# Taking every engine's instructions in source order, in a two-layer encoder trunk on one core

## The chip, the cores and the metric

The kernel runs on one core of a Trainium2 chip. The metric is the device time of one execution in microseconds (us): the median of three runs. The profile is of one further execution of the same program. PE is the TensorE matmul engine (PEld its weight loads), DVE VectorE, ACT ScalarE, POOL GpSimd, SP SyncE, which here only issues transfers.

## What is computed

Two layers on 256 tokens of width 2048 in float32. Each layer is a norm, one input projection, eight retention heads and a gated linear recurrence side by side, an output projection, and a SwiGLU feed-forward part of width 5632; a last norm follows.

```python
for l in range(DEPTH):                               # DEPTH = 2
    h = _rmsnorm(x, norm1_g[l])
    p = (h @ w_in[l]).astype(f32)
    q, k, v, g, xb, yb = jnp.split(p, ...)           # 5 x 1024 wide, and yb
    o_ret = _retention(q, k, v, g, ret_gn_g[l])      # 8 heads of 128
    o_lru = _rg_lru_branch(xb, yb, ...)              # conv, gates, scan over time, gelu, norm
    x = x + jnp.concatenate([o_ret, o_lru], -1) @ w_out[l]
    h = _rmsnorm(x, norm2_g[l])
    x = x + (jax.nn.silu(h @ ffn_w_gate[l]) * (h @ ffn_w_up[l])) @ ffn_w_down[l]
return _rmsnorm(x, final_g)
```

## The kernel before

**Split products.** A weight comes from memory as float32 (`raw`, loads of up to 1 MB issued by SP, three buffers). ACT makes of it `whi`, a copy in the engine's reduced format, and DVE makes `wlo = raw - whi` (lines 557 and 558, in `split`). Activations are pairs of the same kind, made by `pair` (lines 126 to 130). A product is then one matmul of 512 columns with `whi` and one of 256 with `wlo` (lines 193 and 195) per piece of 128 of the contraction.

**Units and ticks.** The work is a list of units, one per weight slot, and the loop at the end of `trunk` walks it. In a layer, units 0 to 7 are the v projection, which uses lines 438 to 440. Units 8 to 47 are the other projections, 16 pieces each: for the recurrent channel group n = 0 to 7 its x is unit 8 + 4n and its y unit 9 + 4n, and two units of heads (q, k, g in turn) follow. The heads that are left come after n = 7, so that units 38 to 47 are g4, q5, k5, g5, q6, k6, q7, k7, g6, g7. Units 48 to 63 are the output projection, and the feed-forward part follows in three thirds of gate, up and down units. A unit of four blocks is written like this: at blocks 0, 1 and 2 a third of the split of the unit two further on, then the block's eight matmuls, then a tick; after the last block the unit's `done`. "(25, block 3)" means the tick after block 3 of unit 25.

```python
for b, block in enumerate(u.blocks):
    ...                      # split(n + 2, part) at blocks 0, 1, 2
    block()
    tk.tick()
if u.done:
    u.done()
```

**What follows the stream.** `tk.after(d, fn)` hangs a step of a branch d ticks behind. For a head: `scores` (PE) five ticks after k is done, `decayed` (DVE, writes `sT`) one later, `weighted` (PE) two later, `moments` (DVE, then two operations on POOL) one later, `normed` (DVE, writes `on`) two later, `turned` (PE transposes) two later, `gated` (DVE, ACT, DVE) one later. For a channel group: `x_done` (ACT `low`, DVE `z` and `xb`, ACT `xc`, DVE three times), `gates` (PE) eight ticks later, `decays` (five operations on ACT) one later, `inputs` (DVE) two later; after an odd n `roots` (ACT) for both groups one later and both `scan`s one later, each of DVE operations with a square on ACT between them. `y_done` (DVE, ACT), `cubic` (DVE, ACT) and `gelu` (DVE) hang on the y unit. With the scan of n = 7 come the `sums` of `yr` two ticks later (PE, DVE `rc`, POOL), `rows` four ticks later (DVE `dg`, PE, ACT), and eight `scaled` from six ticks on (each DVE, ACT, DVE). `softplus`, a run of small dependent operations on DVE (lines 567 to 586), is written for tick 29.

**Order.** The framework fixes, when the program is built, in which order each engine takes its instructions. Source order is its priority, but by its own estimate of when operands are there it puts later instructions ahead of those that would wait. Waits between engines are semaphores; on its engine an instruction waits for those before it.

Of the kernel before, what the change touches and what calls it, by code (L numbers as in the profile page):

```python
# [29 lines left out]
GELU = math.sqrt(2.0 / math.pi)  # L30
# [18 lines left out]


class Ticks:
    """Work that follows the stream of large products, some ticks behind."""

    def __init__(self):
        self.now = 0
# [13 lines left out]


class Unit:
    """One slot of a weight: its source, its width, its products, what follows."""

    def __init__(self, src, width, blocks, done=None, begin=None):
        self.src, self.width, self.blocks = src, width, blocks
# [4 lines left out]
@with_exitstack  # L80
def trunk(ctx: ExitStack, tc, a, out):
    nc = tc.nc
    pool = lambda name, bufs, **k: ctx.enter_context(tc.tile_pool(name=name, bufs=bufs, **k))
    const = pool("const", 1)
    raw_p = pool("raw", RAW)
# [12 lines left out]
    def tmp(tag, n=T, dtype=F32):  # L98
        return (two_p if tag in TWO else one_p).tile([P, n], dtype, tag=tag, name=tag)

    def small():
        return sm_ps.tile([P, 512], F32, tag="sm", name="sm_ps")

    # ---- constants and parameters
    par = const.tile([P, NPAR], F32, name="par")
    rot = const.tile([P, 2, T], F32, name="rot")
    ones = const.tile([P, P], F32, name="ones")
# [2 lines left out]
    n4sp = const.tile([P, DEPTH * NL], F32, name="n4sp")  # L110
# [7 lines left out]
    units = []  # L118
    st = {}

    # ---- pieces of the layers
    def pair(x_ap, scale=None):
        """x (times a column or a number) as two float32r parts whose sum is exact."""
        t = op_p.tile([P, 2, T], F32R, tag="op", name="op")
        if scale is None:
            S.activation(out=t[:, 0, :], in_=x_ap, func=AF.Copy)  # L126
            V.tensor_tensor(out=t[:, 1, :], in0=x_ap, in1=t[:, 0, :].bitcast(F32), op=ALU.subtract)  # L127
        else:
            S.activation(out=t[:, 0, :], in_=x_ap, func=AF.Copy, scale=scale)  # L129
            V.scalar_tensor_tensor(  # L130
                out=t[:, 1, :], in0=x_ap, scalar=scale, in1=t[:, 0, :].bitcast(F32),
                op0=ALU.mult, op1=ALU.subtract,
            )
        return t

    def sums(parts, n, key):
        """1 / sqrt(sum over partitions and parts / n + eps), a column for each half of the tokens."""
        ps = small()
        for j in range(2):
            for i, x in enumerate(parts):  # L140
                PE.matmul(ps[:, j : j + 1], lhsT=x[:, j * P : (j + 1) * P], rhs=ones[:, 0:1],
                          start=i == 0, stop=i == len(parts) - 1)
        rc = two_p.tile([P, 2], F32, tag="rc", name="rc")
        V.tensor_scalar(out=rc, in0=ps[:, 0:2], scalar1=1.0 / n, scalar2=EPS, op0=ALU.mult, op1=ALU.add)  # L144
        G.tensor_tensor(out=rc, in0=rc, in1=mhalf, op=ALU.pow)  # L145
        st[key + "c"] = rc

    def spread(key):
        """The same as a row on every partition, in PSUM."""
        dg = one_p.tile([P, 2, P], F32, tag="dg", name="dg")  # L150
        ps = small()
        for j in range(2):
            V.tensor_scalar(out=dg[:, j, :], in0=ident, scalar1=st[key + "c"][:, j : j + 1], scalar2=None, op0=ALU.mult)
        for j in range(2):
            PE.matmul(ps[:, j * P : (j + 1) * P], lhsT=ones, rhs=dg[:, j, :], start=True, stop=True)  # L155
        return ps[:, :T]
# [13 lines left out]
            V.tensor_tensor(out=st[key], in0=st[key], in1=sq, op=ALU.add)  # L170

    def joined_halves(ps):
        """The two halves of a sum of products, added."""
        low, z = tmp("low"), tmp("z")
        S.activation(out=low, in_=ps[:, T : 2 * T], func=AF.Copy)  # L175
        V.tensor_tensor(out=z, in0=ps[:, 0:T], in1=low, op=ALU.add)  # L176
        return z

    def column_unit(src, n_k, operand, done, begin=None, order=None):
        """128 output features, all tokens: n_k pieces of the contraction."""  # L180
        u = Unit(src, n_k * P, [], begin=begin)
        order = order or list(range(n_k))

        def block(i):
            ks = order[i : i + 4]

            def run():
                if i == 0:
                    u.ps = big_ps.tile([P, 512], F32, tag="big", name="acc_ps")
                for k in ks:  # L190
                    w = slice(k * P, (k + 1) * P)
                    x2 = operand(k)
                    PE.matmul(u.ps, lhsT=u.hi[:, w], rhs=x2.rearrange("p a t -> p (a t)"),  # L193
                              start=k == order[0], stop=False)
                    PE.matmul(u.ps[:, T : 2 * T], lhsT=u.lo[:, w], rhs=x2[:, 0, :],  # L195
                              start=False, stop=k == order[-1])
            return run

        u.blocks += [block(i) for i in range(0, n_k, 4)]
        u.done = lambda: done(u.ps)  # L200
        return u

    # ---- retention
    def rotary(ps, name):
        z = joined_halves(ps)
        t, u, o = tmp("rt"), tmp("ru"), tmp(name)
# [7 lines left out]
    def head(l, h):  # L214
        c = {}

        def g_done(ps):
            """2 silu(g) = g (1 + tanh(g / 2))"""
            z = joined_halves(ps)
            V.tensor_tensor(out=z, in0=z, in1=st["rs"], op=ALU.mult)  # L220
            c["g"] = tmp("sg")
            S.activation(out=c["g"], in_=z, func=AF.Tanh, scale=0.5)
            V.scalar_tensor_tensor(out=c["g"], in0=c["g"], scalar=1.0, in1=z, op0=ALU.add, op1=ALU.mult)
            tk.after(1, turned)
# [72 lines left out]

        return q_done, k_done, g_done

    # ---- recurrent branch  # L300
    def lru(l, n):
        c = {}
        i = l * NL + n
# [26 lines left out]
            tk.after(1, decays)  # L330

        def decays():
            """r, i = (1 + tanh(./2)) / 2;  log a = n4sp (1 + tanh);  1 - a^2 = -tanh(log a) (1 + a^2)"""
            r, g, at, tl, w = tmp("lr"), tmp("lg"), tmp("la"), tmp("lt"), tmp("lw")
            n4 = n4sp[:, i : i + 1]
            S.activation(out=r, in_=c["g_ps"][:, 0:T], func=AF.Tanh, scale=0.5, bias=hb[:, 0, i : i + 1])
            S.activation(out=g, in_=c["g_ps"][:, T : 2 * T], func=AF.Tanh, scale=0.5, bias=hb[:, 1, i : i + 1])
            S.activation(out=at, in_=r, func=AF.Exp, scale=n4, bias=n4)
            S.activation(out=tl, in_=r, func=AF.Tanh, scale=n4, bias=n4)
            S.activation(out=w, in_=at, func=AF.Square)  # L340
            c.update(t=tl, g=g, a=at, w=w)
            tk.after(2, inputs)
# [34 lines left out]
            tk.after(1, cubic)  # L377

        def cubic():
            """2 gelu(y) = y (1 + tanh(GELU (y + 0.044715 y^3)))"""  # L380
            y2 = c["y2"]
            V.tensor_scalar(out=y2, in0=y2, scalar1=0.044715, scalar2=1.0, op0=ALU.mult, op1=ALU.add)
            V.tensor_tensor(out=y2, in0=y2, in1=st["y", l, n], op=ALU.mult)
            S.activation(out=y2, in_=y2, func=AF.Tanh, scale=GELU)
            tk.after(1, gelu)

        def gelu():
            y = st["y", l, n]
            V.scalar_tensor_tensor(out=y, in0=c["y2"], scalar=1.0, in1=y, op0=ALU.add, op1=ALU.mult)
# [8 lines left out]

        return x_begin, x_done, y_done

    # ---- norms between the blocks
    def residual(k, ps):
        V.tensor_tensor(out=X[:, k, :], in0=ps[:, T : 2 * T], in1=X[:, k, :], op=ALU.add)  # L403
        V.tensor_tensor(out=X[:, k, :], in0=ps[:, 0:T], in1=X[:, k, :], op=ALU.add)  # L404

    def after_residual(k, nxt, gains):
        """Chunk k of the residual is new: its part of the next norm and operand."""
        accumulate("xa", X[:, k, :], k == 0)
        st[nxt, k] = pair(X[:, k, :], gains(k))
        if k == KD - 1:  # L410
            tk.after(2, lambda: sums([st["xa"]], D, "rs"))
            tk.after(4, lambda: rows("rs"))
# [5 lines left out]
        st["rot"] = r  # L418

    def v_units(l):  # L420
        """All tokens of half of v, 4 pieces of the contraction to a slot."""
        res = []
        for g in range(2):
            hold = {}
# [35 lines left out]
    def layer_units(l):  # L460
# [12 lines left out]
            for _ in range(REC_AFTER[n] if n < NL - 1 else len(heads)):  # L473
                res.append(heads.pop(0))

        # output projection; the last head is the last to be ready
        order = [0, 1, 2, 3, 4, 5, 6] + list(range(8, 16)) + [7]
        for n in range(KD):
            def done(ps, n=n):
# [11 lines left out]
                u.split_at = (4, 4, 4)  # L491
            res.append(u)

        # feed-forward
        for t, (f0, nf) in enumerate(THIRDS):
            for f in range(f0, f0 + nf):
                c = {}
# [32 lines left out]
    for l in range(DEPTH):  # L530
        units += layer_units(l)
# [31 lines left out]
    sp = [const.tile([P, nl], F32, name=f"sp{j}") for j in range(4)]  # L563

    def softplus():
        """-4 softplus(-lam), with log1p(e) = 2 artanh(e / (2 + e))"""
        lam = par[:, i0 : i0 + nl]
        V.tensor_scalar(out=sp[0], in0=lam, scalar1=-1.0, scalar2=None, op0=ALU.mult)
        V.tensor_tensor(out=sp[1], in0=sp[0], in1=lam, op=ALU.max)
# [14 lines left out]
            b0 = PARAMS[name][0]  # L584
            V.tensor_scalar(out=hb[:, j, :], in0=par[:, b0 : b0 + nl], scalar1=0.5, scalar2=None, op0=ALU.mult)

    # the first operands come with the first weights, a quarter at a time
    V.memset(ones, 1.0)
    V.memset(mhalf, -0.5)
    warm = small()  # L590
# [68 lines left out]


def _columns(w, k0=0, nk=None):
    """[L, K, N] -> [L, N / 128, 128 (k in its piece), pieces * 128]"""
    L, K, N = w.shape
    w = w.reshape(L, K // P, P, N // P, P)[:, k0 : (k0 + nk if nk else None)]
    w = w.transpose(0, 3, 2, 1, 4)
    return np.ascontiguousarray(w).reshape(L, N // P, P, -1)
# [48 lines left out]
```

## Time and profile before

| | us |
|---|---|
| median of three runs | 2266.14 (2265.61 to 2266.22) |
| profiled execution, its span | 2262.9 |
| PE busy in the span | 2239.7 (99%) |
| DVE busy | 1530.3 (68%) |
| ACT busy | 1160.7 (51%) |
| POOL busy | 85.3 (4%) |
| memory traffic | 186 GB/s over the span |

The profiled execution's own time is its span and what lies around it. The span is 3.2 us under the median of the runs. Busy times come from one execution; idle times carry the engine or transfer that ended them. The ends of matmuls are modelled by the profiler, so that starts are the safer numbers on PE.

### The profile page before, as it was taken

How to read it: one execution, taken by the hardware profiler on the slowest of the kernel's cores; microseconds unless marked ns; L12 is line 12 of the kernel's file. 1: busy time of each engine (PE TensorE's matmuls, PEld its weight loads, DVE VectorE, ACT ScalarE, POOL GpSimd, SP SyncE). 2: the span in 40 equal slices, each digit the busy share in tenths (PEclk: the TensorE clock that was granted, in tenths of full speed). 3: DMA queues.
4: the chain of work that ended last, by engine and by line, in shares of the span. 5: the costliest groups of instructions: out<-in, count | busy, mean ns of one | idle time of the engine just before them, and what ended most of it. 6: DMA issues, size and time to landing. Idle time of an engine off the chain costs nothing.

```text
span 2262.9 us, 32580 instructions
## 1 busy us (share of the span) xinstructions
PE 2239.7 (99%) x12748; PEld 1949.9 (86%) x12748; DVE 1530.3 (68%) x2818; ACT 1160.7 (51%) x2040; POOL 85.3 (4%) x128
## 2 busy tenths in 40 slices
PE   8999999999999999999999999999999999999997
PEld 6888888888888888888888888888888888888886
DVE  8788877666566666666758889776665666566665
ACT  5666644555344543445546765455543455444553
POOL 4001110000000000000000101000000000000000
PEclk9999999999999999999999999999999999999999
DMA  7455455555555555555555554555555555555553
GB/s 254 176 177 197 179 177 186 187 192 192 188 189 189 192 185 198 186 189 184 191 200 179 180 192 168 180 186 188 195 184 194 187 190 192 185 196 186 189 182 114
DMA packets 63721, 422.96 MB, mean 187 GB/s; under 512 B 7376, under 2 KB 8016, under 8 KB 25168
## 3 DMA queue, kind: packets, MB, share of 16 engines
q1 hardware_dynamic: 61200, 414.60, 51.7%
q0 software_dynamic: 1792, 5.24, 0.8%
q8 instruction: 99, 1.62, 0.3%
q10 hardware_dynamic: 576, 1.05, 0.1%
q14 instruction: 54, 0.44, 0.1%
HBM read 418.77 MB, written 2.10 MB: 186 GB/s over the span
## 4 chain that ended last, share of the span: by engine, by line
PE 97%; DVE 1%; DMA 1%; issue 0%; POOL 0%; ACT 0%; SPq 0%; DVEq 0%; POOLq 0%
PE acc_ps L193 61%; PE acc_ps L195 31%; PE v_ps L439 1%; PE v_ps L438 1%; PE v_ps L440 1%; PE sm_ps L328 1%; DVE wlo L558 1%; DMA x<-in_x_dram 0%; PE sm_ps L237 0%; DVE op L130 0%; DMA raw<-in_w_v_dram 0%; PE sm_ps L155 0%; PE sm_ps L286 0%; DVE x L642 0%; PE sm_ps L238 0%
## 5 line engine op out<-in xcount | busy, mean ns | idle before, releaser
L193 PE MATMUL acc_ps<-op,whi 128*128 128x512 f32 x6016 | 2105.6, 396 | 0.0
L195 PE MATMUL acc_ps<-op,wlo 128*128 128x256 f32 x6016 | 1672.9, 278 | 0.0
L193 PEld LDWEIGHTS acc_ps<-op,whi 128*128 128x128 f32 x6016 | 1128.8, 188 | 263.3
L558 DVE TENSOR_TENSOR wlo<-raw,whi 128x683 fp32r<-128x683 f32 (+5 forms) x1204 | 1007.5, 851 | 458.4 <-ACT whi L557 457.4
L557 ACT ACTIVATE whi<-raw 128x683 fp32r<-128x683 f32 (+5 forms) x1204 | 860.8, 754 | 853.3 <-PE acc_ps L193 765.7
L195 PEld LDWEIGHTS acc_ps<-op,wlo 128*128 128x128 f32 x6016 | 1131.5, 188 | 0.7
L403 DVE TENSOR_TENSOR x<-acc_ps,x 128x256 f32<-128x256 f32 x128 | 54.3, 424 | 219.1 <-PE acc_ps L195 219.1
L176 DVE TENSOR_TENSOR z<-acc_ps,low 128x256 f32<-128x256 f32 x256 | 107.1, 419 | 2.2 <-ACT low L175 2.2
L175 ACT ACTIVATE low<-acc_ps 128x256 f32<-128x256 f32 x256 | 93.9, 367 | 9.2 <-PE acc_ps L195 9.2
L126 ACT ACTIVATE op<-mix 128x256 fp32r<-128x256 f32 x104 | 43.4, 417 | 71.9 <-DVE mix L507 68.9
L502 ACT ACTIVATE sg<-z 128x256 f32<-128x256 f32 x88 | 36.8, 418 | 67.5 <-DVE z L501 67.5
L145 POOL TENSOR_TENSOR rc<-rc,mhalf 128x2 f32<-128x2 f32 x7 | 7.7, 1096 | 1684.8 <-DVE rc L144 1684.8
L439 PE MATMUL v_ps<-wlo,op 128*128 128x512 f32 x128 | 52.3, 409 | 7.5 <-DVE wlo L558 7.5
L404 DVE TENSOR_TENSOR x<-acc_ps,x 128x256 f32<-128x256 f32 x128 | 54.3, 424 | 4.3
L438 PE MATMUL v_ps<-whi,op 128*128 128x512 f32 x128 | 51.6, 407 | 1.2 <-ACT op L129 1.2
L440 PE MATMUL v_ps<-whi,op 128*128 128x512 f32 x128 | 51.7, 404 | 0.1
L127 DVE TENSOR_TENSOR op<-mix,op 128x256 fp32r<-128x256 f32 x104 | 43.5, 419 | 0.2
L439 PEld LDWEIGHTS v_ps<-wlo,op 128*128 128x128 f32 x128 | 25.3, 197 | 15.0 <-DVE wlo L558 10.1
L506 DVE TENSOR_TENSOR sg<-sg,rs 128x256 f32<-128x256 f32 x88 | 36.9, 420 | 0.8 <-ACT sg L502 0.8
L507 DVE TENSOR_TENSOR mix<-z,sg 128x256 f32<-128x256 f32 x88 | 36.9, 419 | 0.0
L501 DVE TENSOR_TENSOR z<-z,rs 128x256 f32<-128x256 f32 x88 | 36.9, 419 | 0.0
L130 DVE SCALAR_TENSOR_TENSOR op<-x,par,op 128x256 fp32r<-128x256 f32 x64 | 34.3, 539 | 0.2 <-ACT op L129 0.2
(114 smaller groups left out, 729.5 us busy)
## 6 DMA issues: line engine op xcount, KB each, us to landing
raw<-in_w_gate_dram SPq DMA_DIRECT2D x88, 1024.0 KB, 4.8
raw<-in_w_up_dram SPq DMA_DIRECT2D x88, 1024.0 KB, 4.8
raw<-in_w_in_dram SPq DMA_DIRECT2D x80, 1024.0 KB, 4.8
raw<-in_w_down_dram SPq DMA_DIRECT2D x64, 960.0 KB, 4.7
raw<-in_w_out_dram SPq DMA_DIRECT2D x32, 1024.0 KB, 4.8
raw<-in_w_down_dram SPq DMA_DIRECT2D x32, 896.0 KB, 4.5
raw<-in_w_v_dram SPq DMA_DIRECT2D x12, 1024.0 KB, 4.7
raw<-in_w_v_dram SPq DMA_DIRECT2D x16, 256.0 KB, 6.5
```

What stands on the lines that cost most here:

```text
L127: V.tensor_tensor(out=t[:, 1, :], in0=x_ap, in1=t[:, 0, :].bitcast(F32), op=ALU.subtract)
L175: S.activation(out=low, in_=ps[:, T : 2 * T], func=AF.Copy)
L176: V.tensor_tensor(out=z, in0=ps[:, 0:T], in1=low, op=ALU.add)
L193: PE.matmul(u.ps, lhsT=u.hi[:, w], rhs=x2.rearrange("p a t -> p (a t)"), start=k == order[0], stop=False)
L195: PE.matmul(u.ps[:, T : 2 * T], lhsT=u.lo[:, w], rhs=x2[:, 0, :], start=False, stop=k == order[-1])
L403: V.tensor_tensor(out=X[:, k, :], in0=ps[:, T : 2 * T], in1=X[:, k, :], op=ALU.add)
L404: V.tensor_tensor(out=X[:, k, :], in0=ps[:, 0:T], in1=X[:, k, :], op=ALU.add)
L438: PE.matmul(ps, lhsT=x2[:, 0, t], rhs=u.hi[:, w], start=k == 0, stop=False)
L439: PE.matmul(ps, lhsT=x2[:, 0, t], rhs=u.lo[:, w], start=False, stop=False)
L440: PE.matmul(ps, lhsT=x2[:, 1, t], rhs=u.hi[:, w], start=False, stop=k == KD - 1)
L557: S.activation(out=u.hi[:, w], in_=u.raw[:, w], func=AF.Copy)
L558: V.tensor_tensor(out=u.lo[:, w], in0=u.raw[:, w], in1=u.hi[:, w].bitcast(F32), op=ALU.subtract)
```

## The change

One line enters a mode of the framework in which no engine's instructions are reordered: each engine gets them in the order in which the source emits them. Semaphores, buffers, operations and their operands stay. The rest of the diff takes out comments and docstrings.

```diff
 def trunk(ctx: ExitStack, tc, a, out):
     nc = tc.nc
+    ctx.enter_context(tc.manual_schedule())
     pool = lambda name, bufs, **k: ctx.enter_context(tc.tile_pool(name=name, bufs=bufs, **k))
     const = pool("const", 1)
     raw_p = pool("raw", RAW)
```

## Rows read from the trace of the kernel before

**Rows 1.** The page, busy time of each engine (share of the span, instructions).
```profile
PE 2239.7 (99%) x12748; PEld 1949.9 (86%) x12748; DVE 1530.3 (68%) x2818; ACT 1160.7 (51%) x2040; POOL 85.3 (4%) x128
```

**Rows 2.** PE's waits: line, releaser, us in total, times, longest.
```profile
PE v_ps L439 <- DVE wlo L558: 7.5, 6, 3.8
```

**Rows 3.** Four stretches: length, busy us of each engine, clock, DMA.
```profile
16.35:36.70 20.35, 14.09 (x48) 10.18 (x48) 20.21 (x33) 9.83 (x19) 16.44 (x19) 0.83 0.56 197
...
64.80:310.70 245.90, 245.18 (x1414) 214.01 (x1413) 207.14 (x431) 157.78 (x281) 24.19 (x39) 1.00 0.52 182
310.70:2236.00 1925.30, 1924.58 (x11034) 1679.67 (x11034) 1263.40 (x2274) 966.85 (x1696) 29.53 (x43) 1.00 0.53 187
...
143.30:287.80 144.50, 143.78 (x830) 125.25 (x828) 126.16 (x272) 96.28 (x174) 15.91 (x25) 1.00 0.50 178
```

**Rows 4.** PE in order of time: start, us, line, tiles [idle before].
```profile
70.41 0.40 PE L193 MATMUL acc_ps<-op,whi 128*128 128x512 f32 x1
...
143.25 0.48 PE L193 MATMUL acc_ps<-op,whi 128*128 128x512 f32 x1
...
265.19 0.61 PE L141 MATMUL sm_ps<-ones,acc 128*128 128x1 f32 x4
...
287.27 0.30 PE L286 MATMUL sm_ps<-ident,on 128*128 128x128 f32 x1 [0.72 <-DVE on L272]
...
322.37 0.40 PE L193 MATMUL acc_ps<-op,whi 128*128 128x512 f32 x1
...
328.02 0.40 PE L193 MATMUL acc_ps<-op,whi 128*128 128x512 f32 x1
```

**Rows 5.** DVE in order of time, 149 to 173 us.
```profile
149.92 0.87 DVE L558 TENSOR_TENSOR wlo<-raw,whi 128x682 fp32r<-128x682 f32 x1 [0.22 <-ACT whi L557]
150.71 0.42 DVE L176 TENSOR_TENSOR z<-acc_ps,low 128x256 f32<-128x256 f32 x1
...
154.77 0.43 DVE L389 SCALAR_TENSOR_TENSOR y<-y,y 128x256 f32<-128x256 f32 x1 [0.48 <-ACT y L384]
...
157.68 0.42 DVE L208 TENSOR_TENSOR rt<-z,rotl 128x256 f32<-128x256 f32 x1
...
159.00 0.43 DVE L346 SCALAR_TENSOR_TENSOR lg<-lg,xc 128x256 f32<-128x256 f32 x1
...
161.85 0.42 DVE L358 TENSOR_TENSOR lg<-lg,lw 128x256 f32<-128x256 f32 x1
162.31 0.69 DVE L360 TENSOR_TENSOR_SCAN lr<-la,lg 128x256 f32<-128x256 f32 x1
...
171.70 1.53 DVE L319 SCALAR_TENSOR_TENSOR xc<-xb,par,xc 128x256 f32<-128x256 f32 x3
```

**Rows 6.** ACT in order of time, 154 to 159 us.
```profile
154.32 0.42 ACT L384 ACTIVATE y<-y 128x256 f32<-128x256 f32 x1 [1.23 <-DVE y L383]
...
156.58 0.47 ACT L336 ACTIVATE lr<-sm_ps,hb 128x256 f32<-128x256 f32 x1
...
158.59 0.77 ACT L557 ACTIVATE whi<-raw 128x683 fp32r<-128x683 f32 x1
```

**Rows 7.** POOL in order of time, the two operations between `moments` and `normed`.
```profile
284.70 1.13 POOL L264 TENSOR_SCALAR ve<-mv 128x2 f32<-128x2 f32 x1 [7.15 <-DVE mv L262]
285.92 0.76 POOL L265 TENSOR_TENSOR ve<-ve,mhalf 128x2 f32<-128x2 f32 x1
```

**Rows 8.** PE in order of time around its longest idle time.
```profile
19.48 0.80 PE L439 MATMUL v_ps<-wlo,op 128*128 128x512 f32 x1 [3.83 <-DVE wlo L558]
...
20.92 0.63 PE L440 MATMUL v_ps<-whi,op 128*128 128x512 f32 x1
...
25.02 0.39 PE L439 MATMUL v_ps<-wlo,op 128*128 128x512 f32 x1
```

**Rows 9.** ACT and DVE in order of time near the start.
```profile
12.52 0.63 ACT L557 ACTIVATE whi<-raw 128x512 fp32r<-128x512 f32 x1 [0.77 <-DMA raw<-in_w_v_dram]
...
24.15 0.71 DVE L578 TENSOR_SCALAR sp<-sp 128x16 f32<-128x16 f32 x1
```

## The prediction, made before the change was run

> **What bounds the kernel now.** I read the page's busy line first, then PE's waits, then the table of two long stretches, then the engines' instructions in order of time. PE is busy 2239.7 of 2262.9 us, DVE 68%, ACT 51% [rows 1]. PE's own waits add up to little: 7.5 us for `wlo`, all of it at the start [rows 2], 0.72 us a layer for one transpose [rows 4], and some in the tail. So time can only come out of the start; anywhere else the change can at best cost nothing. The reader should see how unlike the two main stretches are [rows 3]. While the projections with their branches run (64.8 to 310.7, and its twin in layer 2), DVE is busy 207.1 of 245.9 us (84%) and ACT 157.8. From there to 2236 DVE has 66%, and in that share lies the whole feed-forward part. An order that makes DVE and ACT wait for each other has room in the second and almost none in the first.
>
> **What the change moves.** No operation is added. On PE nearly nothing moves: the small products already stand at the block ends where the source has them, in both layers, but for three places in each: the sums of `yr` one product into unit 41 (the source: after block 2 of unit 40, nine products earlier), their spread in two pieces in unit 41, and the transposes of head 5 three and five products late, after a wait of 0.72 us [rows 4]. SP issues only weights, in source order already. What moves is DVE and ACT. Today a third of a split slips in between any two dependent steps of a branch. In the source the order in a unit is fixed: third 0, the ticks' work of block 0, third 1, ticks, third 2, ticks, ticks, the unit's `done`. Where a step goes DVE, ACT, DVE, the next `whi` is queued on ACT behind the step that waits for DVE, and DVE's next `wlo` behind that.
>
> **The prices** (DVE's time to get past each piece, start to start, its waiting included). DVE: a third of `wlo` 0.78; a 256-column operation 0.34 where the next is independent, 0.46 where it needs the result; the three of a rotary 1.32, with `z` in front (0.46) and the last (0.34) 2.12; the convolution's three 1.53; a scan 0.72 with its dependent successor; a hop between engines 0.03 [rows 5]. ACT: a `whi` 0.77, a 256-column operation 0.42 of which 0.31 pass before the next may start (my reading of neighbouring starts), the five of `decays` 2.01 [rows 6]. So DVE result, ACT operation, `whi`, `wlo` costs DVE 0.03+0.31+0.77+0.03 = 1.14 of waiting. From these:
> L (third of a split) 0.78; Q (`done` of q or k) 2.12; X (`done` of x: 0.46+0.45+0.63 for ACT's `xc`+1.53) 3.1; Y (`done` of y, wait for `whi` included) 2.02; C (`cubic`: 0.3+0.45+1.14) 1.88; e (`gelu`) 0.34; G (`done` of g) 2.02; P (`gated`: 0.48+1.14) 1.62; M (`moments`) 0.75; N (`normed`) 0.65, 0.5 more where it waits for POOL's two operations of 1.13 and 0.76 [rows 7]; D (`whi` behind `decays` after G) 1.9; I (`inputs`) 0.68; W (`decayed`) 0.47; S (both scans with their squares on ACT, 2×2.41, and 0.36 for `whi`) 5.2; R (`z` behind `roots` on ACT) 0.65; K (one `scaled`: 0.45+0.45+0.34) 1.24.
>
> **The sum for a layer.** Unit by unit in source order, in us:
> 21 X+M+N+3L+0.5: 7.3; 22 Y+C+P+3L: 7.9; 23 Q+I+3L: 5.1; 24 R+Q+S+3L: 10.3; 25 X+W+3L: 5.9; 26 Y+C+e+M+N+3L: 8.0; 27 G+D+P+I+3L: 8.6; 28 Q+3L: 4.5; 29 X+3L: 5.4; 30 Y+C+e+3L: 6.6; 31 as 23: 5.1; 32 R+G+S+W+3L: 10.7; 33 to 35 as 21 to 23: 20.3; 36 as 28: 4.5; 37 as 25: 5.9; 38 as 26: 8.0; 39 as 27: 8.6; 40 as 24 with 0.1 for `rc`: 10.4; 41 Q+3L, `dg` 0.5, 1.7 behind `rs`, 2K: 9.1; 42 G+W+3L+4K: 9.8; 43 Q+M+N+3L+2K: 8.3.
> Together 170.3, and 0.4 for the first `low`: 170.7 us from the start of unit 21 to head 5 being ready for the transposes in unit 44. PE starts unit 21 at 143.25 and has passed these transposes at 288.0, its wait of 0.72 included [rows 4]; at the place where the source has them it is some 142.7 us after 143.25. DVE and ACT are therefore late by 28.0 us. Units 9 to 20 by the same pieces come to 76.4 us; PE takes 143.25-70.41 = 72.8 [rows 4]: 3.6 us more. A lead of two units (5.65 us each [rows 4]) hides lateness of the splits, but not of results that a small product needs two blocks later, so PE stops there. At `weighted` of head 2, the end of unit 25: `decayed` is done after 0.4+7.3+7.9+5.1+10.3 and X+2L+W = 5.1, so at 36.1; PE is there after five units, some 1.9 of small products and 0.7 of waiting for the transposes in unit 22, so at 30.8; it waits 5.3. The same count run on gives 5.6 at `weighted` of head 3 (end of 32), 8.1 at the sums of `yr` (unit 40), 2.3 at their spread, 5.0 at the transposes in unit 44, and some tenths at those of other heads. After that the chain is back within PE's time. 32 us a layer, 64 in all.
> The check on it: DVE is busy 126.2 of 144.5 us there today [rows 3]. The pieces hold that work and some 45 us of waits, where 18 are free.
>
> **The clock.** After PE's longest idle time, 3.83 us, the records of the products last 0.63 us instead of 0.39 until about 23.9 [rows 8], and the granted clock of that stretch is 0.83 on the mean [rows 3]: 4.4 us at the lower of its two levels (1.2 of 2.4 GHz), so 2.2 us lost. Four of the waits are longer. After three of them DVE and ACT are the bound and take the loss in; after the last it counts: 2 us a layer.
>
> **The start.** `softplus` is written for tick 29 but fills DVE from 5.4 us on. From 16.35 to 36.7, where PE last waits, DVE is busy 20.2 of 20.35 us [rows 3], and eleven of those small operations take 4.6 us of it, start to start (one stands in the rows) [rows 9]. Until 16.35 they also kept DVE from unit 1, whose first `whi` was done at 13.15 [rows 9]: 3.1 us more. Against that, PE must still take its products for each of the last pieces, and POOL's sums slow DVE there as before. I take 5 us; between 2 (only the stalls after 16.35 shrink, and the low clock stays) and 7.7. In its own place, unit 7, `softplus` costs some 29 times 0.23 us on a DVE that needs 2.4 of each 5.5 us there: hidden by the lead, which would have to be under 10 us to show it.
>
> **What stays.** In the feed-forward units the same counting gives 4.8 us for a gate and 5.1 for an up, against 5.65 of PE; for the last third's down products 4.9 against 4.94: no loss. The three spreads of `rs` may each make PE wait some 0.3 us: 1 us. The tail, from 2249, is already in source order.
>
> **Rivals.** (1) *The waits mostly overlap*: ACT runs ahead further than I let it, and DVE stops only where even a punctual DVE is late. At the sums: R+Q+L+4.82 = 8.4 us after the start of unit 40, when PE gets there after 4.24: 4.1; the spread 2.3; the transposes 8.34-7.06 (a unit and a block of PE) = 1.3. That is 7.7 a layer: 2266.1+15.4-5+1 = 2277. For it: DVE's plain work fits. (2) *Faster*: the lead covers everything, only the start changes: 2266.1-5 = 2261; it decides if DVE is never more than two blocks (2.8 us) late. Against it: unit 40 alone breaks that. The Trainium skill (Perfetto Trace Analysis, "Identifying the Most-Contended Engine") has one look for the engine with the highest occupancy and work on that first; by that rule PE, whose work stays as it is, would hold the time at this rival's. The rows bear it out for today's order only: DVE's 84% [rows 3] leaves 39 us a layer, and the waits of source order ask for more. (3) *Nothing much moves*, because source order and today's differ too little, or gain and loss cancel: 2266. Against it: DVE's rows show thirds between nearly all dependent steps. (4) *Worse*: the low clock after each wait also falls on PE-bound stretches (four times 2.2 a layer) and the down units with 0.04 us to spare fall behind: 2330+14+16 = 2360.
>
> **How the numbers follow.** The profiled execution's span is 2262.9 us, 3.2 under the median of 2266.14, so the sum is put on the median: 2266.1 + 2×(32+2) - 5 + 1 = 2330. The pieces are good to some 5%, 12 us a layer, since small errors of a sum close to PE's time come out whole. Chances: forecast (2300 to 2350) 0.66; rival (1) 0.15; (2) 0.06; (3) 0.03; (4) 0.10. The range from 2277 to 2360 leaves out (2), (3), and the ends of (1) and (4). A difference of 0.2%, about 4.5 us, is what a measurement of this kernel can tell from none. Slower by more 0.90, within 0.04, faster 0.06.
>
> **What would show it.** In the changed profile: PE waiting for `sT`, `acc`, `dg` and `on` at the places named, in both layers; a granted clock under full in those slices; DVE idle before `wlo` with ACT's `whi` as releaser inside 64 to 350; ACT idle before `sq`, the tanh and `op`, released by DVE; no change in feed-forward; the `softplus` lines after 50 us and `wlo` no longer holding PE at 28 and 36 us. The forecast is wrong if PE shows no wait at the sums of `yr`, or if feed-forward units are longer than 5.65.

## The result, and the profile after

The changed kernel takes 2359.62 us (median of four runs, 2358.17 to 2360.14) against 2265.9 for the kernel before: a ratio of 1.0412, with a 95% interval from 1.0397 to 1.0427. The profiled execution's span is 2357.8 us, 94.9 more than before. Slower, as forecast, but by 94 us and not by 64. Line numbers are one higher than in the kernel before.

The busy line of the page answers [rows 1]. PE has the same 12748 instructions and is busy 37.7 us longer: its records are longer, not more. DVE's 69 us more are not more work. Its 2818 records add up to 1701 us before and 1705 now (`wlo` lasts 851 ns on the mean before and 855 now). Busy time counts records that overlap once, and they overlap less when DVE stands still between two of them. ACT even has 16 instructions fewer: 20 loads of function tables (ACT_TABLE_LOAD, 1.28 us each, which no line of the source names) in place of 36. Eight of the 16 that are gone stood before the square roots of `roots`, which now come in pairs. So the loss is not in the amount of work of any engine.

```profile
PE 2277.4 (97%) x12748; PEld 1968.1 (83%) x12748; DVE 1599.5 (68%) x2818; ACT 1142.0 (48%) x2024; POOL 81.5 (3%) x128
```

PE's waits (line, releaser, us in total, times, longest) answer [rows 2]. The wait for `wlo` at the start has gone; DVE's results of the branches have come in its place.

```profile
PE sm_ps L252 <- DVE sT L245: 27.7, 8, 5.9
PE sm_ps L142 <- DVE acc L171: 17.3, 2, 8.7
PE sm_ps L287 <- DVE on L273: 7.9, 2, 4.0
PE sm_ps L238 <- DVE kT L212: 5.9, 2, 3.0
PE sm_ps L156 <- DVE dg L154: 4.9, 4, 1.8
```

PE in order of time, layer 1 (start, us, line, tiles, idle before). Eight waits stand where [rows 4] has a single one, of 0.72. Layer 2 has them again, each within 0.7 us of layer 1 but for the second, which is 1.98 there (the last row).

```profile
136.64 0.76 PE L238 MATMUL sm_ps<-qT,kT 128*128 128x256 f32 x2 [2.87 <-DVE kT L212]
...
143.71 0.38 PE L252 MATMUL sm_ps<-v,sT 128*128 128x128 f32 x1 [0.37 <-DVE sT L245]
...
180.82 0.80 PE L252 MATMUL sm_ps<-v,sT 128*128 128x128 f32 x2 [5.92 <-DVE sT L245]
...
182.91 0.63 PE L194 MATMUL acc_ps<-op,whi 128*128 128x512 f32 x1
...
185.23 0.39 PE L194 MATMUL acc_ps<-op,whi 128*128 128x512 f32 x1
...
230.22 0.58 PE L252 MATMUL sm_ps<-v,sT 128*128 128x128 f32 x1 [4.91 <-DVE sT L245]
...
289.49 0.56 PE L142 MATMUL sm_ps<-ones,acc 128*128 128x1 f32 x2 [8.67 <-DVE acc L171]
...
296.94 0.38 PE L156 MATMUL sm_ps<-dg,ones 128*128 128x128 f32 x1 [1.82 <-DVE dg L154]
...
311.36 0.49 PE L252 MATMUL sm_ps<-v,sT 128*128 128x128 f32 x2 [1.72 <-DVE sT L245]
...
323.26 0.79 PE L287 MATMUL sm_ps<-ident,on 128*128 128x128 f32 x2 [4.04 <-DVE on L273]
...
1316.26 0.38 PE L252 MATMUL sm_ps<-v,sT 128*128 128x128 f32 x1 [1.98 <-DVE sT L245]
```

The eight of layer 1 sum to 30.3 us. Behind a wait of 5.92 the products of 512 columns last 0.63 us, and 0.39 again from 185.2 on, as in [rows 8].

Four stretches answer [rows 3] (length; busy us and instructions of PE, PEld, DVE, ACT and POOL; granted clock of PE; DMA share and GB/s): the start, units 8 to 47 of layer 1, and the feed-forward products of layer 1 and of layer 2.

```profile
16.00:36.70 20.70, 18.28 (x66) 11.64 (x67) 20.70 (x23) 11.78 (x22) 18.02 (x21) 1.00 0.60 222
...
65.91:356.72 290.81, 260.49 (x1424) 225.03 (x1423) 220.06 (x441) 146.98 (x272) 21.74 (x38) 0.94 0.45 156
...
447.00:1187.80 740.80, 740.80 (x4196) 642.40 (x4195) 477.36 (x792) 350.09 (x613) 0.00 (x0) 1.00 0.54 186
...
1617.47:2344.30 726.83, 726.83 (x4197) 635.38 (x4195) 465.47 (x771) 347.75 (x607) 0.00 (x0) 1.00 0.53 184
```

The two feed-forward stretches hold the same products, at full clock and without idle time of PE, and yet differ by 13.9 us. Before, both took 726.9. In layer 1 the pairs of a 512- and a 256-column product now follow each other at 353.3 ns, in layer 2 at 346.7 as before; 2096 pairs make 13.9 us of it.

Start by start of the units against the trace before: the start gives back 4.5 us; units 8 to 47 take 43.4 more in layer 1 and 41.7 in layer 2; the feed-forward part of layer 1 with its spread 14.4; the feed-forward part of layer 2 nothing. That sums to 95.0 of 94.9.

How a wait arises is seen in unit 22, DVE and then ACT in order of time. DVE's `y` is done, ACT squares it and only then makes the next `whi`, and DVE stands for 1.15 us before `wlo`. Two steps later the same happens with ACT's tanh. The prediction had 1.14 for such a step.

```profile
152.34 0.43 DVE L375 TENSOR_TENSOR y<-z,rs 128x256 f32<-128x256 f32 x1
153.91 0.87 DVE L559 TENSOR_TENSOR wlo<-raw,whi 128x682 fp32r<-128x682 f32 x1 [1.15 <-ACT whi L558]
...
155.02 0.42 DVE L384 TENSOR_TENSOR y<-y,y 128x256 f32<-128x256 f32 x1
156.60 0.87 DVE L559 TENSOR_TENSOR wlo<-raw,whi 128x683 fp32r<-128x683 f32 x1 [1.15 <-ACT whi L558]
```

```profile
152.80 0.42 ACT L377 ACTIVATE y<-y 128x256 f32<-128x256 f32 x1 [2.02 <-DVE y L375]
153.12 0.76 ACT L558 ACTIVATE whi<-raw 128x682 fp32r<-128x682 f32 x1
155.48 0.42 ACT L385 ACTIVATE y<-y 128x256 f32<-128x256 f32 x1 [1.60 <-DVE y L384]
155.80 0.76 ACT L558 ACTIVATE whi<-raw 128x683 fp32r<-128x683 f32 x1
```

### The profile page after: what moved, and what is told of

The parts are those of the page before. It is cut to its first block, busy times and chain, and to the rows that moved or that the text cites. A ratio compares the mean times of both kernels' runs of the same rounds, so it can differ in the third digit from the quotient of the medians.

```text
span 2357.8 us, 32550 instructions
## 1 busy us (share of the span) xinstructions
PE 2277.4 (97%) x12748; PEld 1968.1 (83%) x12748; DVE 1599.5 (68%) x2818; ACT 1142.0 (48%) x2024; POOL 81.5 (3%) x128
## 4 chain that ended last, share of the span: by engine, by line
PE 83%; DVE 10%; ACT 5%; issue 1%; DMA 0%; POOL 0%; SPq 0%; DVEq 0%; ACTq 0%
PE acc_ps L194 53%; PE acc_ps L196 26%; DVE wlo L559 4%; ACT whi L558 2%; PE v_ps L441 1%; PE v_ps L440 1%; PE v_ps L439 1%; DVE z L177 1%; DVE lr L361 0%; DVE op L131 0%; DVE xc L320 0%; ACT L354 0%; DVE y L363 0%; DMA raw<-in_w_v_dram 0%; DVE ru L211 0%
## 5 line engine op out<-in xcount | busy, mean ns | idle before, releaser
L194 PE MATMUL acc_ps<-op,whi 128*128 128x512 f32 x6016 | 2134.1, 400 | 0.0
L559 DVE TENSOR_TENSOR wlo<-raw,whi 128x683 fp32r<-128x683 f32 (+5 forms) x1204 | 970.0, 855 | 235.2 <-ACT whi L558 233.8
L558 ACT ACTIVATE whi<-raw 128x683 fp32r<-128x683 f32 (+5 forms) x1204 | 830.1, 748 | 239.5 <-PE acc_ps L194 185.6
L170 ACT ACTIVATE sq<-x 128x256 f32<-128x256 f32 x59 | 24.7, 418 | 143.2 <-DVE x L405 143.2
L171 DVE TENSOR_TENSOR acc<-acc,sq 128x256 f32<-128x256 f32 x73 | 31.1, 426 | 38.8 <-ACT sq L170 38.8
```

The costliest lines, as they stand in the source:

```text
L558: S.activation(out=u.hi[:, w], in_=u.raw[:, w], func=AF.Copy)
L559: V.tensor_tensor(out=u.lo[:, w], in0=u.raw[:, w], in1=u.hi[:, w].bitcast(F32), op=ALU.subtract)
```

## The experiments

The long spacing comes and goes between runs of one and the same program in six of the kernels below: their times stand in steps of about 14 us. Each layer with the long spacing adds 13.9, so times are compared at the short spacing in both layers; which spacing a run had is shown for the profiled one and inferred from its step for the others. The changed kernel itself is 2359.6 - 13.9 = 2345.7 by that measure, 80 over the kernel before.

### Which engine's order costs the time

```diff
-    ctx.enter_context(tc.manual_schedule())
+    ctx.enter_context(tc.manual_schedule(engines={mybir.EngineType.PE}))
```

> Only PE takes its instructions in source order; DVE, ACT, POOL and SP are ordered as before. Theory (the time goes where DVE and ACT wait for each other): PE's order differs from that of before in three places a layer, and only the sums of yr come early for their operand: in the kernel before DVE finished acc at 265.1 us, and nine products earlier is about 263.7, so 1.4 us a layer, about 1 more for the spread and the transposes: 2266 + 2x2.4 = 2271 (2266 to 2276). Rival (it is PE's own order that costs: a small product at the head of PE's queue holds the large ones behind it): most of the 94 us, so 2330 to 2360.

Measured 2272.02, ratio 1.0027 (1.0016 to 1.0037): 6 us. PE waits 3.2 us for `acc` and 3.0 for `on`. The rival falls.

The same line with `DVE`, with `Activation`, and with both. The engines that are not named, POOL among them, are ordered by the framework.

> Only DVE takes its instructions in source order; ACT, PE and POOL are ordered by the framework. Theory (both engines in source order wait for each other): ACT can put whi ahead of steps that wait for DVE, as in the run with all whi at block 0, so 2305 to 2330 at the short spacing of the feed-forward products, up to 28 more at the long one. Rival (DVE's order alone is the whole cause): 2345 at the short spacing. Rival (ACT's order is the whole cause): 2262 to 2275.

Runs of 2283.01, 2296.30, 2309.53 and 2310.60, ratio of the median 1.015 (1.0091 to 1.021); the profiled run (2310.60) has the long spacing in both layers. At the short one: 2283, 17 us over the kernel before. That lies between the expectations, under the theory's 2305 and over the 2275 of the rival that lays everything on ACT.

> Only ACT takes its instructions in source order; DVE, PE and POOL are ordered by the framework. At the short spacing of the feed-forward products both engines in source order cost some 58 us (2324, PE ordered by the framework) and DVE alone 17 (2283). Theory (each engine's order is cheap while the other can step around it, and the cost comes from the two together): 2264 to 2290, and 13.9 more for each layer at the long spacing. Rival (the costs add up, and most is ACT's): 17 + x = 58, so 2266 + 41 = 2307, 2300 to 2315.

Eight runs from 2269.17 (profiled, short in both layers) to 2300.57, in three steps; ratio 1.0098 (1.0062 to 1.0134). At the short spacing 3 to 7 us. The theory holds: no engine's order alone costs most of the 80.

> DVE and ACT take their instructions in source order, PE and POOL are ordered by the framework. Theory: the waits stay, because what PE waits for is late, and PE can only put a few large products ahead of a late small one: 2340 to 2360, with the waits for sT, acc, dg and on at the same places. Rival (PE's own order costs): 2262 to 2280.

One run of 2323.98 (profiled, short in both layers) and four of 2351.85 to 2352.80; ratio 1.0382 (1.0365 to 1.0399). At the short spacing 58 us, against 17 and about 5 for the two alone. The places were expected wrongly: with PE ordered by the framework the waits are no longer at the small products. PE's waits of that run:

```profile
PE acc_ps L196 <- DVE wlo L559: 16.9, 22, 1.9
PE acc_ps L194 <- ACT whi L558: 14.7, 10, 3.1
PE sm_ps L142 <- DVE acc L171: 5.8, 2, 3.1
```

PE puts large products ahead of a late small one, until the next split is late as well. The last step, to PE (and POOL) in source order as well, is worth 22 of the 80 us. DVE and ACT alone come to 20 to 24; together they cost 58, so 34 to 38 us exist only when both stand in line for each other. PE's order costs 6 alone and 22 on top of both; PE with only one of the two was not run.

### Is it `whi` behind a step that waits for DVE?

```diff
-        S.activation(out=u.hi[:, w], in_=u.raw[:, w], func=AF.Copy)
+        for p in range(parts) if parts == 3 and part == 0 else [part] if parts != 3 else []:
+            h = slice(p * u.width // parts, (p + 1) * u.width // parts)
+            S.activation(out=u.hi[:, h], in_=u.raw[:, h], func=AF.Copy)
```

> Source order on all engines, but the three whi thirds of a split are written at block 0, one after the other, and only the wlo thirds stay at blocks 0, 1 and 2. Theory (DVE is late because its wlo waits for a whi that is queued on ACT behind a step that waits for DVE): at C, P, D and similar steps some 1.1 us of DVE waiting goes, about 15 to 20 times between unit 21 and unit 44, so 17 to 22 of the 28 us of lateness; the waits in the layers fall from 31 us to under 12 each, and the clock loss with them: 2290 (2275 to 2310). Rival (DVE is late by its own dependent steps and by its plain load, ACT is no part of it): 2355 to 2365, the waits as they are.

Runs of 2324.58, 2337.73, 2351.07 and 2353.92 (profiled, long in both layers); ratio 1.0335 (1.028 to 1.0389). At the short spacing some 2325, about 20 less than the changed kernel's 2345.7. Both expectations miss: the effect is there, at about a third of its size. The groups of DVE's instructions between 143.7 and 310 us (busy, mean ns, idle before and its releaser), of the changed kernel, of this one, and, up to 290 us, of the one with DVE alone in source order, tell why:

```profile
L559 DVE TENSOR_TENSOR wlo<-raw,whi 128x683 fp32r<-128x683 f32 (+1 forms) x66 | 55.5, 865 | 19.2 <-ACT whi L558 19.2
L177 DVE TENSOR_TENSOR z<-acc_ps,low 128x256 f32<-128x256 f32 x22 | 9.2, 419 | 7.1 <-ACT low L176 6.8
```

```profile
L561 DVE TENSOR_TENSOR wlo<-raw,whi 128x683 fp32r<-128x683 f32 (+1 forms) x67 | 56.1, 863 | 6.7 <-ACT whi L560 6.7
L177 DVE TENSOR_TENSOR z<-acc_ps,low 128x256 f32<-128x256 f32 x22 | 9.3, 421 | 12.4 <-ACT low L176 12.1
```

```profile
L559 DVE TENSOR_TENSOR wlo<-raw,whi 128x683 fp32r<-128x683 f32 (+1 forms) x65 | 54.3, 862 | 0.0
L177 DVE TENSOR_TENSOR z<-acc_ps,low 128x256 f32<-128x256 f32 x21 | 8.7, 416 | 3.0 <-ACT low L176 3.0
```

With the three `whi` in a row DVE waits 12.5 us less for `whi` but 5.3 more for `low`, which now stands behind them on ACT. With DVE and ACT in source order and PE free, the two waits add up to 23.4 us over the same work (21.6 and 1.8), much as in the changed kernel; with ACT free too they are 3.0. So it is an ACT that may choose which nearly empties both.

### One lateness or several waits?

```diff
-            tk.after(2, weighted)
+            tk.after(5 if h in (2, 3) else 2, weighted)
```

> Source order on all engines; weighted of heads 2 and 3, and what hangs on it, three ticks (4.2 us) later. Theory (one lateness of DVE and ACT that PE pays in instalments wherever it has to wait): the waits for sT of 5.9 and 4.9 us a layer fall under 2 each, and the wait at the sums of yr grows from 8.7 to 16 to 20; time 2350 to 2361. Rival (each wait is a cost of its own, from a step written too close behind its operand): 10.8 us a layer and the slow clock behind them go, nothing grows: 2330 (2325 to 2338).

2360.37 (three runs of 2359.5 to 2360.4, one of 2373.35), ratio 1.0431 (1.04 to 1.0461): the same as the changed kernel, and the rival falls. PE's waits:

```profile
PE sm_ps L287 <- DVE on L273: 26.1, 6, 5.1
PE sm_ps L142 <- DVE acc L171: 17.3, 2, 8.7
PE sm_ps L252 <- DVE sT L245: 9.4, 6, 2.3
```

Of the 27.7 us for `sT` 18.3 are gone, and `on` has grown by 18.2. The theory holds for the sum, not for the place: the next step of the same heads took the waits over, long before the sums of `yr`, which stay at 8.7.

### What does the clock cost?

```diff
+    def filler(ps, n):
+        for _ in range(n):
+            PE.matmul(ps[:, 0:P], lhsT=ones, rhs=ones, start=True, stop=True)
...
+            filler(ps, {2: 26, 3: 21}.get(h, 0))
```

The last line stands in `weighted`; `sums` of `yr` has 38 of them and `turned` of head 5 has 16.

> Source order on all engines, and PE's four long waits of each layer are filled with products of ones by ones that wait for nothing (26 ahead of weighted of head 2, 21 of head 3, 38 of the sums of yr, 16 of the transposes of head 5; 0.21 us each in the first row of such products, so 5.5, 4.5, 8.1 and 3.4 us), written into the bank that the small products behind them write over. Theory A (the clock that falls after each wait costs PE's time): the granted clock stays at full level in these stretches and about 10 us a layer come back: 2340 (2333 to 2345). Theory B (DVE and ACT set the time up to the transposes in unit 44, and PE's slow products lie inside what it would wait anyway): the clock stays up as well, but PE waits longer behind the filler at the next place, and the time stays at 2355 to 2363.

Runs of 2335.52, 2349.45, 2349.72 and 2363.57 (profiled, long in both layers); ratio 1.0349 (1.0312 to 1.0386). At the short spacing 2335.5: 10 us better than the changed kernel, between A and B. Two stretches of this kernel (columns as above), from unit 21 to the transposes of head 5 and around `weighted` of head 2, and the same two of the changed kernel:

```profile
144.96:319.00 174.04, 167.26 (x1026) 147.00 (x1024) 132.72 (x271) 90.52 (x169) 13.69 (x24) 1.00 0.42 148
180.00:190.00 10.00, 9.91 (x63) 8.71 (x62) 7.56 (x18) 4.38 (x7) 2.26 (x5) 1.00 0.40 137
```

```profile
144.40:323.30 178.90, 151.82 (x824) 131.09 (x822) 132.98 (x272) 91.00 (x169) 13.70 (x24) 0.92 0.42 144
181.00:191.00 10.00, 10.00 (x49) 8.88 (x50) 7.01 (x17) 4.85 (x9) 2.24 (x5) 0.80 0.48 145
```

The granted clock is full in both, and from unit 21 to the transposes PE needs 174.0 us and not 178.9. Three small products of this kernel in order of time say where the gain arises:

```profile
230.64 0.49 PE L258 MATMUL sm_ps<-v,sT 128*128 128x128 f32 x2 [1.45 <-DVE sT L250]
...
287.80 0.38 PE L147 MATMUL sm_ps<-ones,acc 128*128 128x1 f32 x2
...
318.97 0.65 PE L294 MATMUL sm_ps<-ident,on 128*128 128x128 f32 x2 [0.45 <-DVE on L279]
```

Behind `weighted` of head 3 comes DVE's `z` of unit 33, in the changed kernel and in this one:

```profile
239.90 0.42 DVE L177 TENSOR_TENSOR z<-acc_ps,low 128x256 f32<-128x256 f32 x1 [1.41 <-ACT low L176]
```

```profile
238.84 0.41 DVE L182 TENSOR_TENSOR z<-acc_ps,low 128x256 f32<-128x256 f32 x1
```

At `weighted` of head 3 nothing is gained (230.64 against 230.22): what the full clock gave in unit 26 is waited for there, as theory B has it. From there on PE's slow products count, as A has it. To the sums it is 57.2 us instead of 59.3: in the changed kernel DVE stands 1.41 us at 239.90 for a unit that PE ran slowly, and here it does not. From the sums to the transposes it is 31.2 us instead of 33.8; in that part DVE itself needs the spread, the scores and `weighted` from PE. Up to the output projection the two layers gain 6.4 and 4.4 us.

### What sets the spacing of the feed-forward products?

```diff
+        for _ in range(fill):
+            PE.matmul(ps[:, 0:P], lhsT=ones, rhs=ones, start=True, stop=True)
         for j in range(2):
             PE.matmul(ps[:, j * P : (j + 1) * P], lhsT=ones, rhs=dg[:, j, :], start=True, stop=True)
```

`fill` is 8 in the spreads of `rs` and 0 in that of `yr`.

> Source order on all engines; eight products of ones by ones stand ahead of the spread of rs, so that PE has no wait between the large products before it and the spread's four products. Theory (the spacing of the 2096 pairs of feed-forward products is set by the instant at which PE restarts after its wait at that spread; without a wait it is always the short one): 346.7 ns in both layers, the feed-forward stretch of layer 1 726.9 us instead of 740.8: 2346 (2343 to 2348) in every run. Rival (the spacing does not hang on that wait): 353.3 ns in layer 1 as before, or runs that differ by steps of 14.

2351.88, all four runs within 2350.91 to 2352.73; ratio 1.038 (1.0362 to 1.0399). The two feed-forward stretches of this kernel:

```profile
448.60:1175.50 726.90, 726.90 (x4196) 635.71 (x4195) 477.10 (x792) 349.99 (x613) 0.00 (x0) 1.00 0.54 189
1608.71:2335.60 726.89, 726.89 (x4197) 635.73 (x4195) 465.35 (x771) 347.54 (x607) 0.00 (x0) 1.00 0.52 183
```

The theory holds for the spacing: 13.9 us are back, and the steps between runs have gone. The time misses its range of 2343 to 2348. Most of that is the fillers' own cost, 1.5 to 1.6 us at each of the three spreads of `rs` from 400 us on, which nothing hides. The spread of `rs` ahead of the feed-forward part, in the kernel before (layer 1), in the changed one (both layers), and in this one:

```profile
407.57 0.61 PE L155 MATMUL sm_ps<-dg,ones 128*128 128x128 f32 x4
```

```profile
446.53 0.71 PE L156 MATMUL sm_ps<-dg,ones 128*128 128x128 f32 x4
...
1617.00 0.71 PE L156 MATMUL sm_ps<-dg,ones 128*128 128x128 f32 x4
```

```profile
448.24 0.61 PE L158 MATMUL sm_ps<-dg,ones 128*128 128x128 f32 x4
```

Where the four products last 0.61 us, nothing held the first one, and the spacing was short, at all 14 such spreads of the seven profiles that have them. Where they last 0.71, PE seems to have been held at the first of them, too shortly to be listed as a wait (DVE worked on `dg` up to 446.67 in layer 1, past the start of the four); both spacings followed, as here in the two layers, the long one at 8 of 14 such spreads. What decides between them was not found.

Two further runs put products of ones by ones behind the last head's transposes, in the kernel with only its start in source order (below).

```diff
             for j in range(2):
                 PE.transpose(ps[:, j * P : (j + 1) * P], c["on"][:, j, :], ident)
+            for _ in range(2 if h == NH - 1 else 0):
+                PE.matmul(ps[:, 256:384], lhsT=ones, rhs=ones, start=True, stop=True)
```

> The kernel with only units 0 to 7 in source order, and two products of ones by ones of 128 columns behind the last head's transposes, ahead of the first 244 pairs of the output projection. Theory (what stands ahead of the first pair sets the spacing of all pairs up to the next small product): the pairs may go from 353.3 to 346.7 ns, so 244 x 6.6 ns = 1.6 us less a layer against 0.2 for the products: 2258.4 (2257.5 to 2259.5); if the two leave the instant at the same point of the pattern, 353.3 ns stays and it is 2261.7. Rival (the spacing belongs to the output projection's operands): 353.3 ns with any number of products.

> As with two extra products, but four, so that the last four small products are as many and as wide as those of the spread behind which the pairs go at 346.7 ns. Theory: 346.7 ns in the first 244 pairs of the output projection of both layers, 2261.3 - 2x(1.6 - 0.45) = 2259.0 (2258 to 2260). Rival (the spacing belongs to the output projection's operands): 353.3 ns, 2262.2.

2262.0 and 2263.13 (ratios 0.9983, 0.9974 to 0.9993, and 0.9988, 0.9978 to 0.9998). The 244 pairs behind them stay at 353.3 ns, 86.5 us in either, and the products cost 0.7 and 1.9 us. So products put there do not change it. The rival falls too: in the run with ACT alone in source order the same pairs of layer 2 went at 346.7.

### The start, and the feed-forward part alone

```diff
+    order = ExitStack()
+    order.enter_context(tc.manual_schedule())
...
     for n, u in enumerate(units):
+        if n == 8:
+            order.close()
```

> Source order on all engines up to the end of unit 7, then the framework's order as before. Theory: the start gains 4.5 us as in the changed kernel and the rest is as before: 2261.5 (2259 to 2264), PE without the waits for wlo at 28 and 36 us. Rival (the gain of the start is given back later, since PE is then ahead of DVE): 2265 to 2267. If the feed-forward pairs of products lock to the longer spacing in a layer, that layer adds 14.

2261.26, ten runs from 2259.97 to 2262.45, ratio 0.9979 (0.997 to 0.9989). The start's gain stays, and this kernel beats both.

```diff
+        if n in (8, 208):
+            order.close()
+        if n in (66, 266):
+            order.enter_context(tc.manual_schedule())
```

Units are counted through both layers here; the mode is closed again ahead of the tail.

> Source order on all engines everywhere but in units 8 to 65 of each layer (the projections with their branches, the output projection and the first gate and up unit, with the spread of rs), where the framework orders as before; it also orders the tail. Theory (all of the loss arises in units 8 to 47, and the feed-forward part loses only by the spacing that PE takes up at that spread): feed-forward units as before, 346.7 ns in both layers, and the start's 4.5 us gained: 2261.5 (2259 to 2264) in every run. Rival (source order makes DVE or ACT late in feed-forward units too): PE waits for wlo there, 2265 to 2290.

2261.31, ratio 0.998 (0.997 to 0.9989), ten runs within 2 us, both feed-forward parts at 346.7 ns, and no wait of PE for `wlo`. In the feed-forward units source order costs nothing.

## Why the prediction was right and wrong

Of the 31 us by which the span grew more than forecast, 13 are the spacing in the feed-forward part, 10 the pieces and 7 the clock (each beyond what the forecast had for it). That 2359.62 lies inside the outer range, which ends at 2360, is luck: the long spacing came in one layer, and no sum of the prediction had it. Without it the time is 2345.7, inside the forecast's 2300 to 2350.

**Right: the kind and the places of the waits.** `weighted` of head 2: 5.3 forecast, 5.92 measured; of head 3: 5.6 and 4.91; sums of `yr`: 8.1 and 8.67; their spread: 2.3 and 1.82; transposes in unit 44: 5.0 and 4.04; units 9 to 20: 3.6 and 3.24, before `scores` and `weighted` of head 1. Only the 1.72 before `weighted` of head 5 was put among the tenths. Together 30.3 against 32 a layer. The start: 5 forecast, 4.5 measured, with the clock full from 16 to 36.7 us, where [rows 3] has 0.83, and `softplus` from 56.6 us on. The rivals "waits mostly overlap", "faster" and "nothing" fall: PE waits at every place named.

**Mis-sized: the clock, 2 us a layer.** Filling the four long waits gave 6.4 us back in layer 1 and 4.4 in layer 2. The step that failed is "after three of them DVE and ACT are the bound and take the loss in". It held from head 2's `weighted` to head 3's, where 0.1 us came back. It failed from there to the sums (2.1 us), where DVE stands for a unit that PE ran slowly, and from the sums to the transposes (2.6 us), where DVE waits for PE's small products while PE is slow. Each side then passes its lateness on. Behind the transposes 2.1 us came back, as forecast.

**Mis-sized, within the stated 5%: the pieces.** With the waits filled, units 8 to 47 still take 37 us a layer more than before, where the pieces gave 32. From unit 21 to the transposes the forecast had 170.7 us; at full clock it took 174.0. These 3.3 came out whole, as the prediction said small errors would. Units 9 to 20 took 5.6 and 6.0 us more than before in the two layers, and the forecast had 3.6. The clock has no part in that. These are the stretches around `scores` and `weighted` of head 1 in the changed kernel, in layer 1 and in layer 2:

```profile
136.60:144.40 7.80, 7.39 (x35) 6.25 (x35) 7.04 (x13) 3.83 (x8) 0.00 (x0) 0.78 0.63 242
1309.10:1317.00 7.90, 5.83 (x35) 5.00 (x35) 7.14 (x14) 3.77 (x8) 0.00 (x0) 1.00 0.63 237
```

In layer 1 the clock fell, and PE then waited 0.37 at `weighted`. In layer 2 it stayed full, and PE waited 1.98. There the slow products did lie inside what PE would have waited anyway. A layer: 34 forecast, 43.4 and 41.7 measured.

**Failed: "no loss" in the feed-forward part, 14.4 us.** The reason given for no loss was right: DVE and ACT keep up there, as the run with that part alone in source order shows. The 0.3 us put down for each wait at a spread of `rs` was the wrong price, for the wait has a sequel: PE may restart into the longer spacing and hold it for 2096 pairs. The counting took 5.65 for a unit, from a stretch at the longer spacing [rows 4]; the units after the spread had 5.55 before, and these two sizes were not asked about. By the prediction's own sign, units longer than 5.65, layer 1 stands on the line: 16 pairs of 353.3 ns are 5.65 us.

**The rival "worse", 2360,** names the measured time by luck, since much of it has another reason. Its four times 2.2 a layer for the clock is above the 6.4 and 4.4 that came back; its 16 for down units falling behind is not what happened.

**The rule on the busiest engine.** By the Trainium skill (Perfetto Trace Analysis, "Identifying the Most-Contended Engine") one works first on the engine with the highest occupancy, and judges TensorE's headroom by its share of peak and by its weight loads. Going by the weight loads that is PE in both kernels, with 86% before [rows 1] and 83% after, and most of the 80 us came from the order of two engines at 68% and about 50%. The measurement decides: the rule names the engine that loses the time, not the ones that cost it.

## What to carry to other kernels

Before an order by hand replaces a planned one, count the steps that go from one engine to another and back, and ask what is queued behind each on both engines: here source order cost 17 us on DVE alone, 3 to 7 on ACT alone and 58 on both. A wait of PE is to be priced with what follows it, the slow clock and the spacing of the products behind it. In this kernel the slow clock cost nothing that shows in units 9 to 20, where DVE and ACT set the pace, and 4 to 6 us a layer behind them. Where only a part gains from the order of the source, give it to that part: the first eight units alone make 2261.3 us.

## What the hardware showed that was not expected

Pairs of a 512- and a 256-column product went at one of two spacings, 346.7 or 353.3 ns, both at full granted clock and without idle time, and kept it up to the next small product, for as many as 2096 pairs. Behind a spread at which PE was not held the short one came in every profile, 14 times of 14. Behind one at which it was held either came, the long one 8 times of 14, and between runs of one program the time moved in steps of about 13.9 us a layer. What decides is open.
